# The fp32 head of an interleaved rotary embedding: four positions in 16 KB rows instead of two in 8 KB rows

## The chip, the cores and the metric

The kernel runs on one core of a Trainium2 chip. The metric is the device time of one execution in microseconds (us), the median of the runs. A profile is taken of one further execution; its times are counted from the first instruction.

## The reference

The input x is fp32 of shape 8 x 2048 x 16 x 64 (batch, sequence, heads, head dimension), with tables cos and sin of 2048 x 32. Neighbouring elements of the head dimension form a pair that is rotated by the angle of its position:

```python
x_pairs = x.reshape(batch, seq_len, num_heads, head_dim // 2, 2)
x1 = x_pairs[..., 0]
x2 = x_pairs[..., 1]
out1 = x1 * cos - x2 * sin
out2 = x1 * sin + x2 * cos
out = np.stack([out1, out2], axis=-1)   # back to the shape of x, fp32
```

x and the output are 67.1 MB each; the tables are 0.26 MB each.

## The kernel before

**Tiles.** The 2048 positions of one batch row are laid over 128 partitions with K = 16 consecutive positions on each. One position is 16 x 64 = 1024 elements, 4 KB in fp32, so a partition reads one contiguous run of 64 KB of x per batch row. A tile xt holds one whole batch row in bf16 (32 KB per partition). There are NX = 5 such buffers for the 8 batch rows.

**Loads and stores.** `load(b, k0)` (L53 to L56) and `store(b, k1)` (L58, L59) are DMAs issued by GpSimd (POOL). They cast on the way: fp32 in HBM, bf16 in the tile. All of them share queue 0. DMAs issued by SyncE (SP) go through queue 1, don't cast, and are few: the head, the two tables, and the tail.

**Head and tail.** The first HEAD = 2 positions of batch row 0 come as fp32 over the SP queue into a tile `head` (L84: 128 rows of 8 KB), and ScalarE casts them into the first tile (L91). The load of batch row 0 on POOL leaves them out: `load(0, HEAD)` (L87) brings 14 positions, 56 KB per partition. The last TAIL = 4 positions of batch row 7 go the other way: ScalarE casts them to fp32 (L118) and SP stores them (L119, 128 rows of 16 KB), beside the last store of POOL (L112, 12 positions, 48 KB per partition). A one-element copy on ScalarE (L117) writes into the tile of batch row 6 first, so it waits until that row's store has read it. The head, the tail and the work tile of `rotate` share one buffer (tag "work", one copy).

**Tables.** cos and sin follow the head on the SP queue (L85, L86: 2 KB per partition each). VectorE (DVE) makes two bf16 tables of them (L93 to L95): sin with alternating signs, cos doubled.

**Arithmetic.** `rotate(b, k0, k1)` runs three VectorE operations on bf16 for positions k0 to k1: qt = x * s_tab (L74), x = x * c_tab in place (L75), x = x + qt with the two elements of each pair swapped (L80). Batch row 0 is done in two pieces, positions 0 to HEAD and HEAD to 16; the others in one piece.

**Order.** The order is written by hand. SP issues head, cos, sin. POOL issues the loads of batch rows 0 to 4 at the start, and then in its own program order: store 0; a one-element copy `mark` that reads the end of tile 4 and so waits for load 4 (L106); store 1; load 5; store 2; load 6; store 3; load 7; stores 4, 5, 6, 7. A store waits for the L80 of its batch row. Loads 5, 6 and 7 wait for stores 0, 1 and 2, whose buffers they take. An instruction of POOL that waits holds back all that follow it there.

Of the kernel before, what the change touches and what calls it, by code (L numbers as in the profile page):

```python
# [2 lines left out]

# [4 lines left out]


@with_exitstack  # L10
def kernel(
    ctx: ExitStack,
    tc: tile.TileContext,
    x: bass.AP,
    cos: bass.AP,
    sin: bass.AP,
    out: bass.AP,
):
    nc = tc.nc
    fp32 = mybir.dt.float32  # L20
    bf16 = mybir.dt.bfloat16
    mult = mybir.AluOpType.mult
    add = mybir.AluOpType.add

    B, S, H, D = x.shape
    P = 128
    K = S // P
    KP = 16
    D2 = D // 2
    HD = H * D  # L30
    NX = 5
    HEAD = 2
    TAIL = 4


    x_t = x.rearrange("b (p k) h d -> b p k (h d)", p=P, k=K)
    out_t = out.rearrange("b (p k) h d -> b p k (h d)", p=P, k=K)
    cos_t = cos.rearrange("(p k) c -> p (k c)", p=P, k=K)
    sin_t = sin.rearrange("(p k) c -> p (k c)", p=P, k=K)

    consts = ctx.enter_context(tc.tile_pool(name="consts", bufs=1))
    xpool = ctx.enter_context(tc.tile_pool(name="xpool", bufs=NX))
    stage = ctx.enter_context(tc.tile_pool(name="stage", bufs=1))

    cos_sb = consts.tile([P, K * D2], fp32)
    sin_sb = consts.tile([P, K * D2], fp32)
    c_tab = consts.tile([P, K, D], bf16)
    s_tab = consts.tile([P, K, D], bf16)

    mark = consts.tile([1, 1], bf16)  # L50
    tiles = {}

    def load(b, k0=0):  # L53
        if b not in tiles:
            tiles[b] = xpool.tile([P, K, HD], bf16, name="xt")
        nc.gpsimd.dma_start(out=tiles[b][:, k0:], in_=x_t[b, :, k0:])  # L56

    def store(b, k1=K):  # L58
        nc.gpsimd.dma_start(out=out_t[b, :, :k1], in_=tiles[b][:, :k1])  # L59

    def rotate(b, k0, k1):
        nk = k1 - k0
        xp = tiles[b][:, k0:k1]
        qt = stage.tile([P, KP, HD], bf16, name="qt", tag="work")

        def rows(a):
            return a.rearrange("p k (h e) -> p k h e", h=H, e=D)

        def tab(a):
            return dataclasses.replace(  # L70
                a, offset=a.offset + k0 * D, ap=[a.ap[0], [D, nk], [0, H], [1, D]]
            )

        nc.vector.tensor_tensor(out=rows(qt[:, :nk]), in0=rows(xp), in1=tab(s_tab), op=mult)  # L74
        nc.vector.tensor_tensor(out=rows(xp), in0=rows(xp), in1=tab(c_tab), op=mult)  # L75
        q_swap = dataclasses.replace(
            qt, offset=qt.offset + 1, ap=[qt.ap[0], [2, nk * HD // 2], [-1, 2]]
        )
        x3 = xp.rearrange("p k (a j) -> p (k a) j", j=2)
        nc.vector.tensor_tensor(out=x3, in0=x3, in1=q_swap, op=add)  # L80

    with tc.manual_schedule():
        head = stage.tile([P, TAIL, HD], fp32, name="st", tag="work")
        nc.sync.dma_start(out=head[:, :HEAD], in_=x_t[0, :, :HEAD])  # L84
        nc.sync.dma_start(out=cos_sb, in_=cos_t)  # L85
        nc.sync.dma_start(out=sin_sb, in_=sin_t)  # L86
        load(0, HEAD)  # L87
        for b in range(1, NX):
            load(b)

        nc.scalar.copy(out=tiles[0][:, :HEAD], in_=head[:, :HEAD])  # L91
        s2 = s_tab.rearrange("p k (i j) -> p (k i) j", j=2)
        nc.vector.tensor_copy(out=s2[:, :, 0], in_=sin_sb)  # L93
        nc.vector.tensor_scalar_mul(s2[:, :, 1], sin_sb, -1.0)  # L94
        nc.vector.tensor_copy(  # L95
            out=c_tab.rearrange("p k (i j) -> p (k i) j", j=2),
            in_=cos_sb.to_broadcast([P, K * D2, 2]),
        )
        for b in range(B):
            if b == 0:  # L100
                rotate(b, 0, HEAD)
                rotate(b, HEAD, KP)
            else:
                rotate(b, 0, KP)
            if b == 1:
                nc.gpsimd.tensor_copy(out=mark, in_=tiles[NX - 1][:1, K - 1, :1])  # L106
            if b < B - 1:
                store(b)

            if b >= 1 and b - 1 + NX < B:  # L110
                load(b - 1 + NX)
        store(B - 1, K - TAIL)  # L112

        tail = stage.tile([P, TAIL, HD], fp32, name="st", tag="work")
        nc.scalar.copy(out=tiles[B - 2][:1, 0, :1], in_=tiles[B - 1][:1, K - 1, :1])  # L117
        nc.scalar.copy(out=tail, in_=tiles[B - 1][:, K - TAIL :])  # L118
        nc.sync.dma_start(out=out_t[B - 1, :, K - TAIL :], in_=tail)  # L119


# [1 line left out]
_INS = ['x', 'cos', 'sin']  # L123
_OUTS = [((8, 2048, 16, 64), 'float32')]


# [23 lines left out]
```

## Time and profile before

| | |
|---|---|
| device time, median of 3 runs | 317.81 us (317.26 to 318.22) |
| span of the profiled execution, first to last instruction | 315.5 us |
| VectorE busy | 210.3 us |
| ScalarE busy, GpSimd busy | 6.9 us, 11.7 us |
| casting load of a whole batch row, written bytes | 4096 KB, seven times; the first load 3584 KB |
| casting store, to landing (median) | 70.1 us |
| tail store, 2048 KB, to landing | 15.5 us |
| VectorE multiply or add, 16384 elements per partition | 8.69 us |
| HBM read, written | 67.63 MB, 67.11 MB |

The profile gives no other time for the profiled execution than its span; the median of the runs is 2.3 us above that. How to read the profile: the busy row gives each engine's busy time and its share of the span. The slices cut the span into 40 equal parts, and a digit is the busy share in tenths. The queue rows give packets, MB and the share of the time of all 16 DMA engines. An issue row (tile <- tensor, issuing queue, count) gives the size of one transfer in KB as written, and the median time from issue to landing. A row of waits says which engine, at which line, waited for what: total us, times, longest. In windows, a DMA packet counts in the stretch in which it begins, so that a share can be above 1.

### The profile page before, as it was taken

Reading aid. Unit: us, or ns where it says so; the run is one execution under the profiler, and the core shown is the slowest. Engines: PE = TensorE matmul, PEld = TensorE weight load, DVE = VectorE, ACT = ScalarE, POOL = GpSimd, SP = SyncE. Lnnn points to the kernel's source line nnn. Section 1 sums busy time; section 2 is a strip of 40 time slices with the busy share of each in tenths; the row PEclk is TensorE's granted clock in tenths of the full one; section 3 lists DMA queues with packets and bytes.
Section 4 is the critical chain, followed back from the end, with each engine's and each line's share of the span. In section 5 each row is a group of like instructions: output and inputs, shape, how many; then the busy total and the mean of one; then the engine's idle time right before and its main releaser. Section 6 shows DMA issues by size and latency. Waiting matters only on the chain.

```text
span 315.5 us, 125 instructions
## 1 busy us (share of the span) xinstructions
DVE 210.3 (67%) x30; ACT 6.9 (2%) x4; POOL 11.7 (4%) x21
## 2 busy tenths in 40 slices
DVE  0000799999999999999999993899509994000000
ACT  4000000000000000000000000000000000000400
POOL 3000000000000301010000100000000000000000
DMA  9899999999999999999999999999999999999997
GB/s 279 184 261 206 199 220 245 199 199 253 212 199 266 399 449 482 399 332 245 220 399 399 399 199 199 399 532 266 199 241 490 399 399 490 440 399 399 432 432 332
DMA packets 2880, 101.71 MB, mean 322 GB/s; under 512 B 320, under 2 KB 320, under 8 KB 576
## 3 DMA queue, kind: packets, MB, share of 16 engines
q0 software_dynamic: 2304, 98.04, 97.1%
q1 hardware_dynamic: 576, 3.67, 3.0%
HBM read 67.63 MB, written 67.11 MB: 427 GB/s over the span
## 4 chain that ended last, share of the span: by engine, by line
another core or an unknown queue 91%; DMA 1%; ACTq 1%; ACT 1%; issue 0%
DMA st<-in_x_dram 1%; ACTq L145 1%; ACT xt L91 1%; ACT xt L117 0%; ACTq L117 0%
## 5 line engine op out<-in xcount | busy, mean ns | idle before, releaser
L74 DVE TENSOR_TENSOR qt<-xt,s_tab 128x16384 bf16<-128x16384 bf16 (+2 forms) x9 | 69.7, 7743 | 19.1 <-DMA xt<-in_x_dram 18.8
L75 DVE TENSOR_TENSOR xt<-xt,c_tab 128x16384 bf16<-128x16384 bf16 (+2 forms) x9 | 69.7, 7743 | 0.4
L80 DVE TENSOR_TENSOR xt<-xt,qt 128x16384 bf16<-128x16384 bf16 (+2 forms) x9 | 69.7, 7744 | 0.3
L93 DVE CAST s_tab<-sin_sb 128x512 bf16<-128x512 f32 x1 | 0.5, 453 | 33.4 <-DMA sin_sb<-in_sin_dram 33.4
L59 POOL DMA_DIRECT2D out_dram<-xt x8 | 4.3, 534 | 139.9 <-DVE xt L80 139.9
L56 POOL DMA_DIRECT2D xt<-in_x_dram x8 | 4.4, 560 | 72.8 <-DMA out_dram<-xt 72.0
L117 ACT COPY xt<-xt 1x1 bf16<-1x1 bf16 x1 | 0.2, 192 | 288.0 <-DMA out_dram<-xt 288.0
L106 POOL COPY mark<-xt 1x1 bf16<-1x1 bf16 x1 | 2.9, 2929 | 39.6 <-DMA xt<-in_x_dram 39.6
L118 ACT CAST st<-xt 128x4096 f32<-128x4096 bf16 x1 | 3.6, 3598 | 0.0
L91 ACT CAST xt<-st 128x2048 bf16<-128x2048 f32 x1 | 1.9, 1897 | 3.4 <-DMA st<-in_x_dram 3.4
L91 ACT ACT_TABLE_LOAD x1 | 1.3, 1283 | 0.7 <-PEq L134 0.7
L95 DVE CAST c_tab<-cos_sb 128x1024 bf16<-128x1024 f32 x1 | 0.7, 683 | 0.0
L94 DVE TENSOR_SCALAR s_tab<-sin_sb 128x512 bf16<-128x512 f32 x1 | 0.4, 444 | 0.0
L134 POOL MEMSET const-float32-0.0<- 128x1 f32 x1 | 0.1, 100 | 0.2 <-issue 0.2
L134 POOL MEMSET const-bfloat16-1.0<- 128x1 bf16 x1 | 0.1, 102 | 0.0
L134 POOL MEMSET const-float32-1.0<- 128x1 f32 x1 | 0.1, 100 | 0.0
L134 POOL MEMSET const-uint8-127<- 128x1 uint8 x1 | 0.1, 100 | 0.0
## 6 DMA issues: line engine op xcount, KB each, us to landing
xt<-in_x_dram POOLq DMA_DIRECT2D x7, 4096.0 KB, 57.6
out_dram<-xt POOLq DMA_DIRECT2D x1, 6144.0 KB, 47.8
xt<-in_x_dram POOLq DMA_DIRECT2D x1, 3584.0 KB, 22.3
out_dram<-st SPq DMA_DIRECT2D x1, 2048.0 KB, 15.5
st<-in_x_dram SPq DMA_DIRECT2D x1, 1024.0 KB, 4.7
cos_sb<-in_cos_dram SPq DMA_DIRECT2D x1, 256.0 KB, 13.4
sin_sb<-in_sin_dram SPq DMA_DIRECT2D x1, 256.0 KB, 31.7
out_dram<-xt POOLq DMA_DIRECT2D x7, 70.1
```

Source lines behind the costliest of these rows:

```text
L56: nc.gpsimd.dma_start(out=tiles[b][:, k0:], in_=x_t[b, :, k0:])
L59: nc.gpsimd.dma_start(out=out_t[b, :, :k1], in_=tiles[b][:, :k1])
L74: nc.vector.tensor_tensor(out=rows(qt[:, :nk]), in0=rows(xp), in1=tab(s_tab), op=mult)
L75: nc.vector.tensor_tensor(out=rows(xp), in0=rows(xp), in1=tab(c_tab), op=mult)
L80: nc.vector.tensor_tensor(out=x3, in0=x3, in1=q_swap, op=add)
L91: nc.scalar.copy(out=tiles[0][:, :HEAD], in_=head[:, :HEAD])
L93: nc.vector.tensor_copy(out=s2[:, :, 0], in_=sin_sb)
L94: nc.vector.tensor_scalar_mul(s2[:, :, 1], sin_sb, -1.0)
L95: nc.vector.tensor_copy(out=c_tab.rearrange("p k (i j) -> p (k i) j", j=2), in_=cos_sb.to_broadcast([P, K * D2, 2]),)
L106: nc.gpsimd.tensor_copy(out=mark, in_=tiles[NX - 1][:1, K - 1, :1])
L118: nc.scalar.copy(out=tail, in_=tiles[B - 1][:, K - TAIL :])
L145: with _tile.TileContext(nc) as tc:
```

## The change

One constant: the head is four positions instead of two. All that depends on it follows. The SP transfer of L84 has 128 rows of 16 KB (2 MB instead of 1 MB); ScalarE's cast at L91 has 4096 elements per partition instead of 2048; the first load on POOL brings 12 positions instead of 14 (48 KB per partition instead of 56); and the two pieces of batch row 0 on VectorE have 4096 and 12288 elements instead of 2048 and 14336. No instruction is added, taken away or moved to another place in the order of an engine or a queue. The tile `head` has room for TAIL = 4 positions in both versions.

```diff
@@ -29,7 +29,7 @@
     D2 = D // 2
     HD = H * D
     NX = 5
-    HEAD = 2
+    HEAD = 4
     TAIL = 4
```

## The prediction

> **What bounds the kernel now.** I read four views in this order: the page's busy rows and slices, the queues with their issues, the waits, and the windows. From the page:
>
> ```profile
> DVE 210.3 (67%) x30; ACT 6.9 (2%) x4; POOL 11.7 (4%) x21
> DMA  9899999999999999999999999999999999999997
> q0 software_dynamic: 2304, 98.04, 97.1%
> q1 hardware_dynamic: 576, 3.67, 3.0%
> HBM read 67.63 MB, written 67.11 MB: 427 GB/s over the span
> st<-in_x_dram SPq DMA_DIRECT2D x1, 1024.0 KB, 4.7
> cos_sb<-in_cos_dram SPq DMA_DIRECT2D x1, 256.0 KB, 13.4
> sin_sb<-in_sin_dram SPq DMA_DIRECT2D x1, 256.0 KB, 31.7
> ```
>
> No compute engine is busy over 67%, and the 16 DMA engines are busy in all 40 slices. The GB/s row of the page swings between 199 and 532 only because it counts written bytes, and a casting load writes half of what it reads. By the wider side of each transfer the rate is constant: the page has 67.63 + 67.11 = 134.74 MB to and from HBM. Now two stages of the windows view (stretch, length, busy DVE, ACT and POOL with instruction counts, clock, DMA share, GB/s):
>
> ```profile
> 33.40:102.10 68.70, 68.36 (x14) 0.00 (x0) 0.54 (x1) 1.00 1.01 221
> 237.20:295.30 58.10, 26.08 (x3) 0.00 (x0) 0.53 (x1) 1.00 1.00 429
> ```
>
> Loads alone write 221 GB/s, so they read 442 (whole packets are booked where they start, hence a share of 1.01); stores alone write 429. The DMA engines have no idle time in either, busy vector engine or not. The trace's packet records say the same: one row of one partition is one packet (16 transfers x 16 engines x 9 = the 2304 packets of q0: 8 rows and a completion), and on each engine they follow each other without a gap from 1.75 us to the last one's end, 313.8 to 314.3. A 64 KB row takes 2.43 us, a 56 KB row 2.13, a 48 KB row (last store) 1.85, a 16 KB row (tail) 0.61, an 8 KB row (head) 0.31. Per KB that is 38 ns throughout.
>
> So the end is a sum of bytes. It moves only if bytes or their rate change, if the engines start or end otherwise, or if the POOL queue ever runs out of queued transfers. The waits show how far the rest is from that:
>
> ```profile
> ACT xt L117 <- DMA out_dram<-xt: 288.0, 1, 288.0
> POOL xt L56 <- DMA out_dram<-xt: 72.0, 3, 37.6
> DVE s_tab L93 <- DMA sin_sb<-in_sin_dram: 33.4, 1, 33.4
> DVE qt L74 <- DMA xt<-in_x_dram: 18.8, 2, 12.4
> ```
>
> The vector engine cannot begin before sin lands at 33.4, and idles 6.4 + 12.4 us before rows 6 and 7 of the batch. The chain of waits is no help here: it gives 91% to an unknown queue.
>
> **Part 1, the bytes.** On each engine 8 head rows of 8 KB and 8 rows of 56 KB (0.31 + 2.13) become 8 of 16 KB and 8 of 48 KB (0.61 + 1.85): 8 x 2.44 = 19.5 us before, 8 x 2.46 = 19.7 after. The 1.85 is a store's row; scaled from the loads' own 2.13 a 48 KB row takes 1.83, which makes 19.5. **Between 0 and +0.2 us; I take +0.1**, the middle, since both rows are as near. No packet is added. A 16 KB fp32 load isn't in the trace; the 8 KB load and the 16 KB store bound it at 0.61 to 0.62.
>
> **Part 2, the start.** Queue 0's first packet comes late: its first issue is at 1.24 us. The windows (columns as before) show when:
>
> ```profile
> 4.75:5.00 0.25, 0.00 (x0) 0.00 (x0) 0.00 (x0) 1.00 0.68 246
> 5.25:5.50 0.25, 0.00 (x0) 0.05 (x1) 0.00 (x0) 1.00 4.79 1122
> 5.75:6.00 0.25, 0.00 (x0) 0.25 (x1) 0.00 (x0) 1.00 0.00 0
> 7.50:7.75 0.25, 0.00 (x0) 0.00 (x0) 0.00 (x0) 1.00 5.52 1212
> 9.75:10.00 0.25, 0.00 (x0) 0.00 (x0) 0.00 (x0) 1.00 4.96 1090
> ```
>
> The bursts are the long q0 rows of all 16 engines beginning together, first at 5.1 to 5.6, then every 2.2 us. Until 5.1 only the SP queue feeds the engines, and it doesn't run dry: of its 27 packets per engine (head 8 + 1, cos 8 + 1, sin 8 + 1) the records have some 14 or 15 done by then, 12 left. With the larger head more is left, so the stretch is filled as before. The ramp (first 8 KB rows took 0.34 to 1.1 instead of 0.31) is a latency paid once: 0, with 0.4 either way if it scales.
>
> **Part 3, the tables arrive later.** After 5.4 the two queues take turns, one packet each: 2.13 + 0.09 for a 2 KB table row makes the 2.2 us above. Counting turns reproduces this trace: 13 of them from 5.4 end at 33.3 for sin and 14.3 for cos (landed at 33.4 and 1.16 + 13.4 = 14.6). After the change, from 2.05 with a 0.5 us ramp, 5 head rows of 0.61 are done at 5.4; 3 rows, 1 completion and 18 table packets are left, 22 turns. These go beside 8 rows of 1.83, a completion, 8 rows of 2.43, a completion and 4 more rows of 2.43: 14.6 + 19.4 + 9.7 = 43.8, with 3 x 0.61 + 18 x 0.09 = 3.5 of its own. **The head lands near 15, sin near 53**, 19 us later. Bounds: if q0's first packet stands behind SP packets until 7.0, 19 turns, 45; if every one of the 27 turns were shared, about 62. The copy L91 (4096 elements; the nearest row is L118's 3.6 us against 1.9 now) ends by 19, well ahead of sin, which hides it.
>
> *The rule.* The Trainium skill, "DMA: Bandwidth & Descriptors", section "Queues, rings and completion order", lets an engine drain a packet of some 9 to 17 descriptors from a ring before it turns to the next. By that rule the 18 table packets pass in two or three turns, sin would land near 20 and nothing would be late. The trace disagrees where each descriptor is one row: sin's 31.7 us to landing needs single rows. The sum below comes out the same either way.
>
> **Part 4, what that lateness costs.** The vector engine runs without a break from 33.38 to the end of row 5 of the batch (183.63 + 8.69 = 192.3), 158.9 us, the same elements in other pieces. From 52.8 it ends at 211.7; row 6 then waits for nothing (its load landed at 198.7) and ends at 237.9, row 7 starts 0.6 late (load at 237.3) and ends at 264.1 instead of 263.5. What is late next are the stores on POOL, a queue in fixed order, with loads queued behind them:
> - store 0, issued at 61.9: now 81, needed at 102.1 when the five loads have landed.
> - store 1, issued at 105.0 after the mark: now 107 (87.5 + 19.4), needed at 121.7 when store 0 has landed.
> - store 2, issued at 122.2: now 133, needed near 160 behind load 5. Load 6 behind it waits for store 1 (141.0) anyway.
> - stores 3, 4, 5: 159, 185, 212, needed near 199, 237 and 256; store 7 at 264.3, needed at 295.3.
>
> Queue 0 always holds a whole 19 us transfer more than it needs; store 1 is tightest, 15 us to spare. The cover fails when the vector engine starts more than 121.7 - 87.5 = 34 us later, sin beyond 67. All 27 turns give 62, still inside. **Cost 0.** The tail waits for store 6 (L117, 295.3), unchanged.
>
> **Sum.** +0.1 + 0 + 0 + 0 on a span of 315.5; the median, 317.8, stands 2.3 above it, and launch and end around the span don't change: **317.9 us**.
>
> **Rivals.**
> - *Faster, 316.9 and below.* Speaks for it: all 16 last rows of load 4 took 3.0 to 3.5 instead of 2.43 (they start at 98.0 to 98.4), a loss of 0.85 that I can't explain; if the order of work causes it, a vector engine 19 us behind may not meet it: 317.0. Also, where q0 starts later than in this execution, the SP queue (12 short packets, about 1 us) may run dry now and not after; that is worth up to 1 us. Against: the boundary of loads and stores stays, and no gap shows. 13%.
> - *Slower, starved queue.* In the load stage, up to 102 us, the SP queue gets less than every second packet. With two q0 rows per turn the 22 turns need 44 rows, over the 40 of the loads, so sin lands near 100, 67 late; store 0 goes out at 128 instead of before 102: 26 us, 344. It decides from sin at 67 on and costs 1 us per us. Against: the counted turns fit 33.4 within 0.2. 5%. The same loss of 0.85 met twice, or more uneven engine ends, give 318.8 to 319.4: 11%.
> - *The change isn't what it says.* A 16 KB row travels as two 8 KB packets: 9 of 16 done at 5.4, 26 turns, sin near 62, the store rule above still kept: 317.9, inside the forecast.
>
> **How the numbers follow.** Forecast 317.9 at 71%, own range 317.0 to 318.8 (0.3%, about what a measurement of this kernel can tell from no change; three runs of it spread over 317.26 to 318.22). Faster 13%, slower 16%. To hold 8 in 10, the range goes to the stall gone together with a filled gap below (317.9 - 0.85 - 0.65 = 316.4) and the stall met twice with ragged ends above (317.9 + 0.85 + 0.65 = 319.4); the 0.65 is one tail row. The starved queue stays outside.
>
> **What would show it.** Right: sin's idle time at L93 near 53 (45 to 62), st landing near 14, DVE's wait at L74 fallen from 18.8 to under 4, store 1 issued near 107, slices still 9 throughout, last slice as now, span 315.5. Wrong: a slice below 9 between 100 and 130 (starved queue), q1's early packets all done before the bursts begin (no turns), or packets over 2880 (split rows).

## The result

| | before | after |
|---|---|---|
| median of 19 runs each, beside each other | 317.75 us (317.26 to 318.45) | 317.24 us (316.95 to 317.58) |
| profiled execution: own time, span | 317.26, 315.5 us | 316.95, 315.2 us |

The ratio is 0.9981, 95% interval [0.9975, 0.9987]: 0.5 us faster. That is less than 0.3%, but clear of no change, and the forecast was +0.1. The slowest runs fell most: the range shrank from 1.2 to 0.6 us.

The page of the kernel after, in the lines that answer to those shown of before:

```profile
DVE 210.3 (67%) x30; ACT 8.6 (3%) x4; POOL 14.2 (5%) x21
...
DMA  7999999999999999999999999999999999999997
...
q0 software_dynamic: 2304, 97.52, 96.3%
q1 hardware_dynamic: 576, 4.72, 3.9%
HBM read 67.63 MB, written 67.11 MB: 428 GB/s over the span
...
st<-in_x_dram SPq DMA_DIRECT2D x1, 2048.0 KB, 14.5
...
cos_sb<-in_cos_dram SPq DMA_DIRECT2D x1, 256.0 KB, 31.7
sin_sb<-in_sin_dram SPq DMA_DIRECT2D x1, 256.0 KB, 51.3
```

Two positions have moved from queue 0 to queue 1: queue 0 writes 0.52 MB less and queue 1 1.05 MB more (a casting load writes half of what it reads). The HBM bytes are the same, and so are the packets, 2880. The first slice reads 7 and not 9 because a packet counts where it begins; by their overlap with this slice the packets fill 0.75 of it before and 0.76 after. The tables take 18 and 20 us longer to land. The waits after:

```profile
POOL out_dram L59 <- DVE xt L80: 191.1, 8, 77.5
DVE s_tab L93 <- DMA sin_sb<-in_sin_dram: 53.0, 1, 53.0
POOL xt L56 <- DMA out_dram<-xt: 39.0, 3, 19.0
```

VectorE begins at 53.0, its 18.8 us of waiting at L74 are gone, and all eight stores now wait on POOL for VectorE. None of it reaches the end, since the DMA engines go on without a gap. The difference must lie in their rows, so I used the trace's packet records as in the prediction (each engine ends with a completion packet; of the 16 ends I give the mean and the latest). The records don't name the engine, but on an engine each row begins where the one before it ended, so an engine can be followed. Two more profiles of each kernel were taken, below; all six together:

| profile (its time) | last rows of load 4, mean length | store 0 begins, mean | ends, mean | ends, latest |
|---|---|---|---|---|
| before (317.26) | 3.31 us | 101.48 | 314.05 | 314.27 |
| before, 2nd (317.88) | 3.62 | 101.77 | 314.32 | 314.89 |
| before, 3rd (317.95) | 3.72 | 101.72 | 314.28 | 314.97 |
| after (316.95) | 3.00 | 101.24 | 313.80 | 313.95 |
| after, 2nd (317.03) | 2.95 | 101.25 | 313.81 | 314.06 |
| after, 3rd (317.12) | 3.05 | 101.28 | 313.84 | 314.14 |

The three times differ by 0.66 on the mean (317.70 against 317.03), the latest ends by 0.66 (314.71 against 314.05). This is more than the 0.51 of the medians: the three runs of after that were profiled are all below its median. The difference has two parts. **The mean end is 0.40 earlier**, and all of it is there when store 0 begins (101.66 against 101.26): the rows at the change from loads to stores are 0.55 shorter and begin 0.15 later. **The ends are more even**: the latest lies 0.49 behind the mean before and 0.23 after. From its first row of store 0 to its end every engine takes 212.55 or 212.56 us in all six profiles, so both parts are decided ahead of store 0.

Both can be seen in windows, where a row counts in the stretch in which it begins (columns: stretch, length, busy DVE, ACT and POOL, clock, DMA share, GB/s). First the change to stores, in the third profile of before and the first of after:

```profile
98.80:100.80 2.00, 2.00 (x1) 0.00 (x0) 0.00 (x0) 1.00 0.00 0
100.80:101.30 0.50, 0.50 (x1) 0.00 (x0) 0.00 (x0) 1.00 0.00 0
101.30:101.80 0.50, 0.50 (x1) 0.00 (x0) 0.00 (x0) 1.00 3.99 1704
101.80:102.30 0.50, 0.50 (x1) 0.00 (x0) 0.00 (x0) 1.00 0.61 262
102.30:102.80 0.50, 0.50 (x1) 0.00 (x0) 0.00 (x0) 1.00 0.31 131
```

```profile
98.80:100.80 2.00, 2.00 (x1) 0.00 (x0) 0.00 (x0) 1.00 0.00 0
100.80:101.30 0.50, 0.50 (x1) 0.00 (x0) 0.00 (x0) 1.00 3.07 1311
101.30:101.80 0.50, 0.50 (x1) 0.00 (x0) 0.00 (x0) 1.00 1.84 786
```

The share of a stretch, times its length, times 16 engines, over 2.43 us gives the rows that begin: 10 of the 16 first store rows begin before 101.3 after the change and none in this profile of before, where three stragglers begin after 101.8. This pair lies far apart; in the first profile of before three rows begin before 101.3 and none after 101.8. Then the end, again before (third) and after:

```profile
312.50:313.50 1.00, 0.00 (x0) 0.00 (x0) 0.00 (x0) 1.00 0.92 393
313.50:314.00 0.50, 0.00 (x0) 0.00 (x0) 0.00 (x0) 1.00 0.92 393
314.00:314.50 0.50, 0.00 (x0) 0.00 (x0) 0.00 (x0) 1.00 0.09 33
```

```profile
312.50:313.50 1.00, 0.00 (x0) 0.00 (x0) 0.00 (x0) 1.00 1.03 442
313.50:314.00 0.50, 0.00 (x0) 0.00 (x0) 0.00 (x0) 1.00 0.02 0
```

In this profile of after no tail row begins past 313.5 (one does in the third); in this one of before a dozen do, and one more past 314.0.

### The profile page after: what moved, and what is told of

Its sections match the earlier page's. It is cut to its first block, busy times and chain, and to the rows that moved or that the text cites. A ratio compares the mean times of both kernels' runs of the same rounds, so it can differ in the third digit from the quotient of the medians.

```text
span 315.2 us, 125 instructions
## 1 busy us (share of the span) xinstructions
DVE 210.3 (67%) x30; ACT 8.6 (3%) x4; POOL 14.2 (5%) x21
## 3 DMA queue, kind: packets, MB, share of 16 engines
q1 hardware_dynamic: 576, 4.72, 3.9%
## 4 chain that ended last, share of the span: by engine, by line
another core or an unknown queue 88%; DMA 5%; ACT 1%; ACTq 1%; issue 0%
DMA st<-in_x_dram 5%; ACT xt L91 1%; ACTq L145 1%; ACT xt L117 0%; ACTq L117 0%
## 5 line engine op out<-in xcount | busy, mean ns | idle before, releaser
L74 DVE TENSOR_TENSOR qt<-xt,s_tab 128x16384 bf16<-128x16384 bf16 (+2 forms) x9 | 69.7, 7743 | 0.3
L106 POOL COPY mark<-xt 1x1 bf16<-1x1 bf16 x1 | 5.4, 5371 | 19.7 <-DMA xt<-in_x_dram 19.7
L91 ACT CAST xt<-st 128x4096 bf16<-128x4096 f32 x1 | 3.6, 3605 | 13.3 <-DMA st<-in_x_dram 13.3
```

## The experiments

All times are medians in us; ratios are against the kernel before, run beside each (its median was 317.53 to 317.81). Theories are named by letters in the expectations.

**VectorE's start.** Both heads, with VectorE held back until load 2 has landed (62.8 and 62.5 us):

```diff
+        nc.vector.tensor_copy(out=mark2, in_=tiles[2][:1, K - 1, :1])
         nc.vector.tensor_copy(out=s2[:, :, 0], in_=sin_sb)
```

> Head of two positions as before; VectorE's first table cast waits for the end of load 2 (near 62.8 us) in place of sin (33.4), so that its work begins 29 us later than before and 10 us later than after the change; store 1 still keeps some 5 us of cover. Theory V (the gain is VectorE running less beside the loads, whatever the size of the head): as after the change or a little below, 316.9 to 317.3, and no loads above 2.47 us near 66 to 86 us. Theory H (the gain is in the head itself: its bytes or its rows): as before, 317.6 to 317.9. Theory W (the stall of the last load rows belongs to the first write to HBM and only varies by chance): the stall stands at 98 us as before, 317.4 to 317.8.

> Head of four positions, VectorE begins at load 2's landing as in the run with two. Theory V: the same as that run within 0.15 us, 316.9 to 317.3. Theory H: 0.5 below that run, 317.1 to 317.3 against 317.6 to 317.9. Theory W: as that run within the scatter, since the first write is unchanged.

Head of two: 317.70, ratio 0.9999 [0.9991, 1.0007]. Head of four: 317.18, 0.9982 [0.9974, 0.9991]. Holding VectorE back changed neither, and the whole difference stays. Theory V falls: the late VectorE isn't the gain, and it costs nothing.

**Tables ahead of the head.**

```diff
-        nc.sync.dma_start(out=head[:, :HEAD], in_=x_t[0, :, :HEAD])
         nc.sync.dma_start(out=cos_sb, in_=cos_t)
         nc.sync.dma_start(out=sin_sb, in_=sin_t)
+        nc.sync.dma_start(out=head[:, :HEAD], in_=x_t[0, :, :HEAD])
```

> Head of four positions, but cos and sin ahead of it on the SP queue: sin lands near 4 us, the head near 16, so VectorE rotates from near 20 us instead of 53, and runs beside the loads for all of their time. Theory V: the gain goes, 317.7 to 318.2. Theory H: it stays, 317.1 to 317.4. Theory W: no change but by chance, 317.2 to 317.8.

318.92 (318.23 to 319.70), 1.0036 [1.0023, 1.0049]: the largest effect of all, by more than any theory gave, and 1.7 above the kernel after, with the same bytes. The start and the end of its profile:

```profile
3.00:4.00 1.00, 0.00 (x0) 0.00 (x0) 1.00 (x2) 1.00 2.24 539
4.00:5.00 1.00, 0.81 (x3) 0.00 (x0) 0.03 (x1) 1.00 0.18 25
...
313.50:314.00 0.50, 0.00 (x0) 0.00 (x0) 0.00 (x0) 1.00 0.17 66
314.00:314.50 0.50, 0.00 (x0) 0.00 (x0) 0.00 (x0) 1.00 0.15 66
314.50:315.00 0.50, 0.00 (x0) 0.00 (x0) 0.00 (x0) 1.00 0.15 66
315.00:316.50 1.50, 0.00 (x0) 0.00 (x0) 0.00 (x0) 1.00 0.10 44
```

Queue 0 begins at 3.28 here, and on 14 engines the first row of load 0 begins before 4.0. The share of 0.18 in the next stretch is a single row (2.81 / 16): two engines start theirs only at 4.7 and 5.2, and these take 2.81 and 2.43 instead of 1.83. No row of either queue begins between 3.84 and 4.72, so these two engines stood idle before that. They begin load 1 about 2 us behind the others, and at the end they work alone, at a share of 0.10 to 0.17: the mean end is 314.17, the latest 316.65. They never made up what they had lost: in the records every transfer gives each engine the same eight rows.

**A write to HBM early, over the SP queue.**

```diff
+        nc.sync.dma_start(out=out_t[B - 1, :, K - 1, :128], in_=head[:, 0, :128])
         nc.scalar.copy(out=tiles[0][:, :HEAD], in_=head[:, :HEAD])
```

> As before, with one more SP transfer of 128 rows of 512 B from the head tile to HBM at the place that the tail overwrites later, so that the first write to HBM comes in the first 50 us and not at 101; its 64 KB cost about 0.15 us. Theory W: the last rows of load 4 take 2.43 us instead of 3.3, and the time falls by up to 0.85, to 316.9 to 317.4. Theories V and H: the stall stays near 98 us, 317.7 to 318.0.

317.77, 0.9997 [0.9988, 1.0005]; the last rows of load 4 took 3.57. Theory W falls in this form.

**Head size and row size.** HEAD = 1, HEAD = 3 (that constant alone), and four positions in two transfers:

```diff
-        nc.sync.dma_start(out=head[:, :HEAD], in_=x_t[0, :, :HEAD])
+        nc.sync.dma_start(out=head[:, :2], in_=x_t[0, :, :2])
+        nc.sync.dma_start(out=head[:, 2:HEAD], in_=x_t[0, :, 2:HEAD])
```

> Head of one position, 4 KB rows: about 1.3 us of rows for each engine, then the 2 KB table rows, all done before 5 us. Theory S (the time follows the engine that ends last; engines fall apart when queue 0 begins while the SP queue is down to its 2 KB rows or dry): engine ends spread over more than 1 us, 318.0 to 319.0. Theory B (bytes moved off the casting queue, a quarter us per position): 317.95 to 318.05 with ends as even as before. Theory R (rows of 16 KB as such): 317.7, like before.

> Head of three positions, 12 KB rows, 3.7 us of them for each engine, so that they last until queue 0 begins. Theory S: as after the change, 317.1 to 317.35, ends within 0.6 us. Theory B: half way, 317.45 to 317.5. Theory R: nearer to before, 317.5 to 317.7.

> Four positions as two SP transfers of two positions, so rows of 8 KB with the bytes of the change; some 26 turns are left for the SP queue at 5.4 us, so sin lands near 62 and VectorE still hides it. Theory S: as after the change, 317.1 to 317.35. Theory B: the same, 317.2. Theory R: as before, 317.6 to 317.8.

One position: 317.34, 0.9988 [0.998, 0.9997]. Three: 317.26, 0.9987 [0.9978, 0.9995]. Four in 8 KB rows: 317.43, 0.9989 [0.998, 0.9998]. All three gain, the smallest head too. So the gain doesn't grow with the bytes (B falls) and doesn't need 16 KB rows (R falls), and S missed the head of one, which it made slower. In the records, heads of one and three have the shortest rows at the change to stores (2.80 and 2.57) but uneven ends (latest 0.51 and 0.91 behind the mean). The two parts of the gain are separate things. With three positions S missed the ends too: 19 of the 128 head rows were still to begin when queue 0 began, and the ends were uneven all the same.

**Tables out of the way of queue 0's start.** First, cos and sin wait for the head to land:

```diff
         nc.sync.dma_start(out=head[:, :HEAD], in_=x_t[0, :, :HEAD])
+        nc.scalar.copy(out=cos_sb[:1, :1], in_=head[:1, 0, :1])
```

> Head of two positions; cos and sin wait for the head to land (a one-element copy by ScalarE into the cos tile, which cos then overwrites), so that no 2 KB row is under way when queue 0 begins; sin lands near 44. Theory S in the form that the 2 KB rows at the start of queue 0 make engines uneven: 317.1 to 317.4 with ends within 0.6 us, unless the engines run dry for a while before queue 0 begins, which adds that gap. Theories B and R: as before, 317.7.

317.37, but with runs up to 319.09, 1.0002 [0.9988, 1.0016]: inconclusive. Its profile (318.12) has queue 0 begin at 4.57, one first row of load 0 that takes 1.0 too long, and a latest end 1.08 behind the mean. Then, the tables behind load 0 on POOL's queue, with both heads:

```diff
         load(0, HEAD)
+        nc.gpsimd.dma_start(out=cos_sb, in_=cos_t)
+        nc.gpsimd.dma_start(out=sin_sb, in_=sin_t)
```

> Head of two positions; cos and sin go over POOL's queue behind load 0 in place of SP's, so that after the head no row takes turns with the loads, and no 2 KB row is under way when queue 0 begins. sin lands near 25. Theory S (2 KB rows beside the start of queue 0 make engines uneven): 317.0 to 317.3, ends within 0.6 us. Theory R (8 KB rows of the head as such are the loss): as before, 317.6 to 317.9.

> The same with a head of four positions. Theory S: the same as the run with two positions within 0.15 us, since the head's size then sets nothing. Theory R: 0.4 to 0.5 below that run, 317.1 to 317.3.

Two positions: 317.53, runs up to 318.93, 1.0003 [0.9993, 1.0013]. Four: 317.32, up to 317.52, 0.9990 [0.9981, 0.9998]. In their profiles the mean ends are alike (314.29 and 314.32) and the latest are not (315.57 and 314.52). S is wrong that table rows do the harm: with two positions and no table row at all on the SP queue, a first row of load 0 still took 0.88 too long. With four, whose head rows were still under way when queue 0 began, none did. In this pair the rows at the change to stores go the other way: 2.96 with two positions and 3.42 with four.

**Second and third profiles** of before and after, unchanged:

> The kernel before, unchanged, for a second profile: its runs lie between 317.26 and 318.64 and the first profile was of one near 317.3. Theory U (the engines' ends fall apart by chance at the start): time beyond 317.3 shows as a spread of the ends above 0.45 us, with the last rows of load 4 as before (3.3 us on the mean). Theory L (the stall at the end of load 4 varies): it shows as longer last rows on all 16 engines and ends as even as before.

> The kernel after, unchanged, for a second profile; its runs lie between 316.95 and 317.58. Theory U: ends spread by 0.6 us or less and the mean end is that of before. Theory L: last rows of load 4 between 2.8 and 3.2 us, 0.2 to 0.3 below those of before, and the mean end earlier by as much.

> The kernel before, a third profile. If both parts of its loss are its own and not chance, the last rows of load 4 take 3.3 us or more on the mean and the mean end lies at 314.05 or later; the spread of the ends goes with the time beyond that.

> The kernel after, a third profile: last rows of load 4 at 2.9 to 3.15 us on the mean, mean end 313.75 to 313.95, ends within 0.6 us of each other.

They are in the table of the first section. U and L both hold a part: both differences are there each time, and in before both grow with the time.

**Eight positions:**

```diff
-    HEAD = 2
+    HEAD = 8
-        head = stage.tile([P, TAIL, HD], fp32, name="st", tag="work")
+        head = stage.tile([P, HEAD, HD], fp32, name="st", tag="work")
```

> Head of eight positions, 32 KB rows: two thirds of it are still to come when queue 0 begins, sin lands near 54. Theory S (long SP rows under way when queue 0 begins keep the engines even): rows of load 0 without a slow one, ends within 0.6 us, 317.1 to 317.3, no better than four positions. If the gain grew with the bytes of the head: below 317.0.

317.23, 0.9990 [0.9981, 0.9999]; no row of load 0 was slow and the latest end is 0.26 behind the mean. A longer head gives no more.

**Store 0 before load 4** (the mark of L106 left out):

```diff
-        for b in range(1, NX):
+        for b in range(1, NX - 1):
             load(b)
...
             if b < B - 1:
                 store(b)
+            if b == 0:
+                load(NX - 1)
```

> Head of two positions; POOL issues store 0 before load 4, and the mark, which would hold store 1 back until load 4 has landed, is left out. The first change from loads to stores comes near 82 in place of 101. If the stall belongs to the first such change: the last rows of load 3, near 79, are long (3.3 us) and those of load 4 are not, total as before, 317.6 to 317.9. If it belongs to the length of the stretch of loads alone: shorter, 317.3 to 317.5. If it belongs to load 4's own rows: it comes with them, near 118.

317.95, 1.0011 [1.0002, 1.002], so 0.35 slower than the kernel before beside it (317.60), which no theory gave; its profile is of one of its quickest runs (317.70) and doesn't show why. Windows of that profile:

```profile
79.50:81.50 2.00, 2.00 (x1) 0.00 (x0) 0.00 (x0) 1.00 0.00 0
81.50:82.50 1.00, 1.00 (x1) 0.00 (x0) 0.00 (x0) 1.00 2.30 983
...
116.00:118.50 2.50, 2.50 (x1) 0.00 (x0) 0.00 (x0) 1.00 1.03 223
```

The long rows came along: the last rows of load 3 begin at 78.6 to 79.4 and take 3.12 to 3.64 each, with no row begun from 79.5 to 81.5; load 4's last rows, from 118.1 on, take 2.43. No row of loads 5 to 7 takes more than 2.44 in any of the 20 profiles. The stall belongs to the first change from large loads to large stores, and isn't shorter after a shorter stretch of loads.

**A store of queue 0 at the start**, for both heads:

```diff
+        nc.vector.memset(pad, 0.0)
+        nc.gpsimd.dma_start(out=out_t[B - 1, :, K - 1, :128], in_=pad)
         load(0, HEAD)
```

> Head of four; POOL's first transfer is a casting store of 128 rows of 128 zeros to a place that the tail overwrites later, so queue 0's first store comes at the start and not at 101 us. If the stall belongs to the first store of queue 0: the last rows of load 4 take 2.43, the time falls by up to 0.55 to 316.7 to 317.0. If it belongs to the first large change from loads to stores on all engines: rows of 3.0 us as after, 317.2 to 317.4.

> The same with a head of two. If the stall belongs to the first store of queue 0 and goes, what is left against the run with four is the spread of the ends alone, 0.2 to 0.4 us: 316.9 to 317.3. If it stays: rows of 3.3 to 3.7 us as before, 317.6 to 317.9.

Four: 317.14, 0.9988 [0.9979, 0.9997]; two: 317.60, 1.0003 [0.9994, 1.0012]. The stall stays, 2.84 and 3.38, so it isn't the first store of the queue either. The pair shows one thing more. In this order sin landed at 32.9 with the head of four, as early as it did in the kernel before, and the gain is still there:

```profile
DVE s_tab L96 <- DMA sin_sb<-in_sin_dram: 32.9, 1, 32.9
```

**Slow rows of load 0 and uneven ends.** Over all 20 profiles of before, after and the variants, the largest excess of a row of load 0 over the usual length goes with how far the latest end lies behind the mean:

| profiles | largest excess in load 0 | latest end behind the mean |
|---|---|---|
| four positions ahead of the tables or with these on queue 0 (7), eight (1) | 0.00 to 0.12 us | 0.15 to 0.44 us |
| two positions, tables behind the head on SP (7) | 0.04 to 0.60 | 0.22 to 0.84 |
| two positions, tables late or on queue 0 (2) | 0.88, 1.00 | 1.28, 1.08 |
| one, three positions (2) | 0.24, 0.21 | 0.51, 0.91 |
| four positions, tables first (1) | 0.99 | 2.48 |

The correlation over the 20 is 0.85, and the lag is there by 23 us: the first rows of load 1 begin within 0.52 to 0.98 us of each other in the three profiles of before, within 0.35 to 0.46 in those of after. Following the engines shows that a slow row makes the late engine: in the five profiles with two positions that have an excess above 0.5, the slow row is its engine's first of load 0, and this engine is the one that ends last. Smaller lags have other sources as well: in the second profile of before half of the 0.57 comes only between load 1 and store 0.

## Why the prediction was wrong

- **Part 1, the bytes: held.** Rows of 0.61 to 0.64 (16 KB, past the first ones, which took up to 1.6) and 1.83 (48 KB) took the place of 0.31 and 2.13; HBM bytes and packets are the same.
- **Part 3, the turns: held.** The head landed at 15.3 (forecast 15), sin at 53.0 (53).
- **Part 4, the lateness: held.** Stores 0 to 4 were issued at 81.5, 107.4, 133.6, 159.8 and 186.0 (81, 107, 133, 159, 185), row 7 of the batch began at 238.1 (237.9), store 7 was issued at 264.6 (264.3). The cost was 0, also with VectorE held back to 62.8. The starved queue did not come, and rows were not split.
- **The frame of the sum failed, and with it the larger part of the gain.** "The end is a sum of bytes" lets a row's time depend on its bytes alone. It carried the long last rows of load 4 over as they were: a change of 0, with no reason given. They took 3.55 us on the mean before and 3.00 after, with the same bytes, and this -0.55 is larger than any other term. What comes ahead of them cost +0.15, against the +0.1 of the sum, and so the mean end moved by -0.40.
- **Part 2, the start: failed.** I said that the stretch is "filled as before" and priced the start at 0, with 0.4 either way for the ramp alone. Filled it was, but not alike: with two positions a row of load 0 on some engine often ran long, with four ahead of the tables none by more than 0.12 us. The kernel ends with the engine that lost most, and its lag behind the mean fell by 0.26, the rest of the 0.66. I had one profile of before, of the fastest run, whose ends lay within 0.44 us (its own time is 317.26, 1.8 above its span of 315.5; the 2.3 of the sum set the median beside the span of the fastest run). The spread of the three runs (317.26 to 318.22) was the sign that something varied.
- **The rival "faster" named the other 0.40 and gave the wrong cause.** I saw the long last rows of load 4, 0.85 too long, and gave 317.0 should a late VectorE not meet them. They did shrink, but not for that: with two positions a late VectorE gains nothing, and with four and queue 0's first store at the start VectorE is as early as before and the gain stays. Its other half, an SP queue that runs dry, isn't it either: in the three profiles of before 11 to 13 of its 27 packets per engine were left at 5.4.

**What stays open.** Why the rows at the first change from loads to stores are shorter after than before, which is the larger part of the gain. It is neither the first HBM write, nor queue 0's first store, nor the length of the stretch of loads, nor VectorE's start. It isn't the head's size as such either: heads of one, three and eight have short rows, but so have the two runs with two positions and the tables moved (2.97 and 2.96), and four positions with the tables on queue 0 have long ones (3.42). And what makes a row of load 0 slow when no long row is under way was not isolated; that a long row hides the wait for queue 0's first data is my reading, not a measurement.

No version beat the kernel after clearly; four positions with queue 0's first store at the start (317.14) or with VectorE held back (317.18), and eight positions (317.23), lie within its range.

## What to carry to other kernels

In a kernel bound by the DMA engines, count per engine and look at when each of them ends: equal shares of bytes didn't make equal ends here, and an engine that fell behind in the first microseconds stayed behind (2.5 us with the tables first). Try the transfer with long rows first on the second queue and the short-row transfers behind it; that order was worth 1.7 us here, the head's size 0.5. Bytes alone don't fix a row's time either: rows of the same bytes took 2.43 us, and 2.6 to 3.7 on the mean at the first change to stores. Before a change of no bytes is forecast at nothing, take the scatter of the runs for a cost that the change may move.

## What the runs showed of the hardware

- Queue 0's start went with what the SP queue had in front: with the loads issued from 1.24 us on, its first row began at 3.28 with the tables' 2 KB rows in front, 4.22 with a head of one, 5.1 with two, 5.6 with three, 5.4 to 5.5 with four, 5.9 with eight. With two positions and the tables out of the way it began at 4.6.
- The one-element copy `mark` on POOL ended with the VectorE instruction that ran beside it. Timeline of the kernel after:

```profile
98.44 8.69 DVE L80 TENSOR_TENSOR xt<-xt,qt 128x16384 bf16<-128x16384 bf16 x1
101.80 5.37 POOL L106 COPY mark<-xt 1x1 bf16<-1x1 bf16 x1 [19.74 <-DMA xt<-in_x_dram]
107.16 8.69 DVE L74 TENSOR_TENSOR qt<-xt,s_tab 128x16384 bf16<-128x16384 bf16 x1
```

And of the kernel before:

```profile
96.31 8.69 DVE L75 TENSOR_TENSOR xt<-xt,c_tab 128x16384 bf16<-128x16384 bf16 x1
102.11 2.93 POOL L106 COPY mark<-xt 1x1 bf16<-1x1 bf16 x1 [39.64 <-DMA xt<-in_x_dram]
```

After the change it starts at 101.80 and ends at 107.17 with VectorE's addition (107.13); before, it took 2.93 and ended at 105.04 with a multiply (105.00). The Trainium skill, "SBUF — State Buffer", section "Who interferes with whom", says that a VectorE instruction with two SBUF inputs contends with a GpSimd instruction that reads SBUF, for ports that are under an exclusive lock; both traces agree. Here it cost nothing: after the change store 1 waited for that addition anyway, and before it was issued at 105.0 and not needed until store 0 had landed at 121.7.
